# Batch-normalised matmul: chunk 11 of the turned x copied apart by GpSimd, one raw block of the third group sent the ordinary way

## The chip, the core and the metric

One core of one Trainium2 chip. The number that counts is the device time of one execution of the program, in microseconds (us). The core's engines are named as the profile names them: PE (TensorE, matmuls; PEld its weight loads), DVE (VectorE), ACT (ScalarE), POOL (GpSimd) and SP (SyncE, which only issues DMAs here). Matmuls write to PSUM, eight banks of 128 x 512 f32; everything else lives in SBUF.

## The reference

x is 16 x 512 x 1024, the weight 1024 x 768, both f32, so that y has 8192 rows and 768 columns. Every column is normalised over all 8192 rows:

```python
y = np.matmul(x, weight)
mean = np.mean(y, axis=(0, 1), keepdims=True)
var = np.var(y, axis=(0, 1), keepdims=True)
return (gamma * (y - mean) / np.sqrt(var + eps) + beta).astype(np.float32)
```

## The kernel before

**Tiles.** The 8192 rows are 16 chunks (c = 0 to 15) of 512 rows. The 768 columns are six tiles nt of 128. Tiles 0 and 1 are done together as the "first group" (256 columns, rows in the PSUM partitions, lines L509 to L671, for chunks 14 and 15 L813 to L826); tiles 2 to 5 are done one by one with the columns in the partitions, eight matmuls of 128 x 512 for each chunk (`col_unit`, L574). A tile can be normalised only when all 16 chunks of it have been multiplied and their statistics gathered, so its normalisation and its stores run beside the matmuls of the next tile, and only the last tile's stand alone at the end.

**x.** GpSimd issues the loads of x (L402), which cast it to bf16. VectorE turns each chunk (L427, L434) into a tile `xT_sb`, so that k lies in the partitions. In most chunks the turning moves 32-bit words, so that two neighbouring k (e = 0 and 1) stay side by side: the tile is `[P, JW, CH, 2]`, and a matmul on one e reads every second bf16 element. Chunks 2, 3 and 6 (`SINGLE`) are turned as single bf16 elements, slower on VectorE (L427), and are contiguous for each e. Chunks in `PARTED` (4, 5, 7 to 10) are copied apart by ScalarE (`part_chunk`, the copies are L546, four of 128 x 1024 for a chunk) into contiguous tiles `x_pl`. Chunks 12 to 15 (`LATE`) are copied apart just before tile 4, by VectorE or ScalarE, whichever the planner finds free. Chunk 11 isn't copied: tiles 2 to 5 read it from `xT_sb`. Chunks 0 to 3 are done for all tiles while x is still being loaded.

**After a matmul.** For a chunk of a tile, VectorE takes statistics (bn_stats, L710; for chunks 4 to 15 of tile 2 ScalarE does it instead, L719 and L723), and ScalarE moves y to SBUF as bf16 (L714), which frees the bank. The first group is summed by VectorE (L661, L665) and GpSimd (L665), merged (L794, L799), summed over the partitions on PE (L870), and brought to a scale and a shift: VectorE L879 to L882 (mean and variance of the sums), L820 (bn_stats of chunks 14 and 15), L886, ScalarE's root, then VectorE L893 to L898. PE spreads them over the partitions (L902). Two pairs of chunks' blocks (chunks 14 and 15) are then normalised by VectorE (L1063) and turned by PE (L1073); the other 14 by VectorE's product (L936) and an addition, on GpSimd for most (L941). GpSimd's additions of L665 and L799 are all that the change's words "behind its additions for the first group" mean.

**Tiles 2 to 4** go out in blocks of two chunks, in one of three ways. The ordinary way of tiles 2 and 3 (`col_block` in mode `xact`): normalise in place (ScalarE L1022 for tile 2, VectorE L1025 for tile 3), turn by a DMA transpose (L1219), ScalarE casts to f32 (L1231), SP stores (L1201). Tile 4 is normalised by VectorE too, and turned by PE between matmuls (L1043), cast by ScalarE (L1209). A *raw* block (`RAW`) is turned by DMA before it is normalised (L1105), for the chunks 0 to 3 while no store runs yet; once scale and shift are known they are spread along the free dimension (L1140 to L1157, seven small copies on GpSimd or ScalarE), VectorE multiplies (L1173), GpSimd adds (L1177), SP stores (L1181).

**The order.** Nothing is ordered by the hardware across engines but what semaphores say; on each engine, the order is fixed by `arrange`, a planner that runs when the program is built. It has a cost and a due time for each task and simulates the engines; a task may name two engines. Buffers (`Slot`) are given out in planned order from pools: eight banks, 12 places for `xT_sb` (`xts`), 29 for y (`ys`), 3 for squares (`sqs`), and a ring for x, turned blocks and results. So a small edit can reorder work far from it. `S` is the planned time at which the first group's matmuls end; `merges` are the last additions of the first group; `clock[0]` is the planned time of PE.

```python
def part_chunk(c, now, engines, small=False, step=0.0, after=()):
    slots = [Slot(sqs if jw < SQ else ys) for jw in range(JW)] if small else [Slot(xts)] * JW
```

A `small` copy lies in three places of `sqs` and one of `ys` in place of one whole `xts` place.

Of the kernel before, what the change touches and what calls it, by code (L numbers as in the profile page):

```python
# [227 lines left out]
def kernel(  # L228
# [20 lines left out]
    NT = N // P  # L249
# [3 lines left out]
    C = M // CH  # L253
# [9 lines left out]
    EARLY = 4  # L263
# [11 lines left out]
    PARTED, LATE, SINGLE = (4,5,7,8,9,10), (12,13,14,15), (2,3,6)  # L275
    MODE = {2:'xact',3:'xact',4:('pe',)*8}
    MODE = {nt: m if isinstance(m, tuple) else (m,) * (C // GY) for nt, m in MODE.items()}
    RAW, RAWADD, RAWDUE = {2:(0,2),3:(0,2),4:(0,2,4)}, {2:'POOL',3:'POOL',4:'POOL'}, {2:14.0,3:8.0,4:8.0}
    RING = 3 * CH // 32 * KQ // 2
    ENG = {"ACT": nc.scalar, "DVE": nc.vector, "POOL": nc.gpsimd, "SP": nc.sync}  # L280

# [11 lines left out]
    def seq(bi):  # L293

        ins = bi.ins
        prev = last.get(ins.engine)
        if prev is not None:
            tc.add_manual_dep(
                ins, prev,
                mybir.DependencyInfo(mybir.DependencyClass.NoSync, mybir.DependencyReason.DATA),  # L300
                reason="order",
            )
        last[ins.engine] = ins.name
        return bi
# [50 lines left out]
    def task(prio, engines, emit, deps=(), lock=False, **kw):  # L355
        t = Task(prio, engines, emit, deps, **kw)
        t.lock = lock
        tasks.append(t)
        return t
# [20 lines left out]
    w_ready, x_ready, x_slot, plain, last_loads = {}, {}, {}, {}, []  # L380
# [66 lines left out]
    for kind, n, *n1 in order:  # L447
# [24 lines left out]
        for i in range(rows // QR):  # L472
            c, q = divmod(m0 // QR + i, QPC)
# [9 lines left out]
        if rows % QR:  # L483
            t0 = rows // QR * QR // 32
            m1 = m0 + 32 * t0
            c, q = divmod(m1 // QR, QPC)
# [40 lines left out]
    def part_chunk(c, now, engines, small=False, step=0.0, after=()):  # L527

        src = x_slot[c]
        slots = [Slot(sqs if jw < SQ else ys) for jw in range(JW)] if small else [Slot(xts)] * JW  # L530
        ts = []

        def copy(jw):
            def emit(eng):
                if small:
                    if jw < SQ:
                        x_pl = sqpool.tile([P, 2, CH], bf16, tag="sq")
                    else:
                        x_pl = ypool.tile([P, 2, CH], bf16, tag="y")
                    slots[jw].tile = [x_pl]  # L540
                elif jw == 0:
                    x_pl = xtpool.tile([P, JW, 2, CH], bf16, tag="xT")
                    slots[0].tile = [x_pl[:, i] for i in range(JW)]
                dst = slots[jw].tile[0 if small else jw]
                pairs = src.tile[:, jw].rearrange("p m e -> p e m")
                seq(nc.scalar.copy(dst, pairs) if eng == "ACT" else ENG[eng].tensor_copy(dst, pairs))  # L546
            return emit

        for jw in range(JW):
            new = small or jw == 0  # L550
            ts.append(task(
                now + step * jw, engines, copy(jw), [x_ready[c, q, JW] for q in range(QPC)] + list(after) + ([] if new else ts[:1]),
                len(engines) > 1, uses=[src] + ([] if new else [slots[jw]]), takes=[slots[jw]] if new else []))
        plain[c] = slots, ts, small
# [71 lines left out]
    def col_unit(nt, c, jws, q0=0, q1=QPC):  # L626
        slot = bank_of.setdefault((nt, c), None) or Slot(banks)
        bank_of[nt, c] = slot
        first = jws[0] == 0 and q0 == 0
        xs = [plain[c][0][jw] for jw in jws] if c in plain else [x_slot[c]]  # L630
        kw = {"takes": [slot], "uses": xs} if first else {"uses": [slot] + xs}
        t = pe_task((1.728 if c in plain or c in SINGLE else 1.808) * len(jws) / JW * (q1 - q0) / QPC,
                    mm(nt, c, list(jws), slot, q0, q1),
                    waits(jws, c, q0, q1) + ([plain[c][1][jw] for jw in jws] if c in plain else []), (nt, c), **kw)
        if q1 - q0 == QPC:
            t.hosts = 4
        if jws[-1] == JW - 1 and q1 == QPC:
            col_stats(nt, c, slot, t)
        return t
# [60 lines left out]
    col_end = {}  # L700
# [88 lines left out]
    merges = []  # L789
# [70 lines left out]
    S = clock[0]  # L860
# [237 lines left out]
    def raw_turn(nt, c, due):  # L1098

        yslot, slot = y_of(nt, c), Slot(ys)  # L1100

        def xbar(eng):
            r_sb = ypool.tile([P, GY * RT, P], bf16, tag="y")
            slot.r = r_sb
            bi = nc.sync.dma_start_transpose(slot.r, y(nt, c, GY))  # L1105
            if not gated:
                tc.add_manual_dep(
                    bi.ins, gate.ins.name,
                    mybir.DependencyInfo(mybir.DependencyClass.Sync, mybir.DependencyReason.DATA),
                    reason="behind the loads",  # L1110
                )
                gated.append(bi)
            seq(bi)

        b = task(due, {"SP": (1.4, 1.4)}, xbar, [col_end[nt, c + i][1] for i in range(GY)] + [gate], dma=XBAR,
                 takes=[slot], uses=[yslot])
        raw[nt, c] = slot, b
# [8 lines left out]
    def raw_spread(nt, fin_task):  # L1126
        bank = Slot(banks)
        k = sorted(RAW).index(nt)
        acc, at = ((sum2, 0), (sum2, 2 * P), (sum3, 2 * P))[k]
        row = acc[:, at:at + 2 * P].rearrange("p (i n) -> p i n", n=P)  # L1130
        wide, turned = sum1[:, NA + 64 * k:NA + 64 * (k + 1)], sum3[:, 64 * k:64 * (k + 1)]
        both = turned.rearrange("p (i n) -> p i n", n=32)
        now = clock[0] + RAWDUE[nt] + 2.0

        def quadrant(i):
            return slice(32 * i, 32 * i + 32)

        def turn(eng):
            for i, src in enumerate((scale, shift)):
                seq(nc.vector.tensor_copy(wide[:, quadrant(i)], src[:, nt:nt + 1].to_broadcast([P, 32])))  # L1140
            seq(nc.vector.transpose(turned, wide))

        def move(eng, dst, src):
            seq(nc.scalar.copy(dst, src) if eng == "ACT" else nc.gpsimd.tensor_copy(dst, src))  # L1144

        def gather(eng):
            for i in range(4):
                move(eng, row[0:32, :, quadrant(i)], both[quadrant(i)])

        def deal(eng):  # L1150
            for i in range(1, 4):
                move(eng, row[quadrant(i)], row[0:32])

        def keep(eng):
            a_ps = psum.tile([P, CH], f32, tag="b")
            bank.tile = a_ps
            seq(nc.scalar.copy(a_ps[:, 0:2 * P], row.rearrange("p i n -> p (i n)")))  # L1157

        d = task(now, dve(0.35), turn, [fin_task], True)
        g = task(now, {"POOL": (0.8, 0.85), "ACT": (0.9, 1.0)}, gather, [d])  # L1160
        s = task(now, {"POOL": (1.2, 1.25), "ACT": (1.0, 1.1)}, deal, [g])
        t = task(now, act(0.4), keep, [s], takes=[bank])
        raw_aff[nt] = bank, t, s, row[:, 1]
# [97 lines left out]
    STEP = {2: 1.9, 3: 2.3, 4: 2.3}  # L1261
    CHUNKS = {nt: list(range(EARLY, C)) for nt in range(GA, NT)}
    if LATE:
        late = [c for c in range(EARLY, C) if c in LATE or c + 1 - c % 2 * 2 in LATE]
        rest = [c for c in range(EARLY, C) if c not in late]
        CHUNKS[NT - 3], CHUNKS[NT - 2] = late + rest, rest + late
    for nt in range(GA, NT - 1):
        if nt == NT - 2:
            for i, c in enumerate(LATE):
                part_chunk(c, clock[0] + 0.0 + 4.0 * i, {"DVE": (0.63, 0.7), "ACT": (1.05, 1.1)},  # L1270
                           i == 0, 4.0 / 4, [col_end[NT - 3, late[-1]][1]])
        for c in CHUNKS[nt]:
            for jws in halves if nt > GA or c > EARLY + 2 else [[jw] for jw in range(JW)]:
                col_unit(nt, c, jws)
        for c in RAW.get(nt, ()):
            if c >= EARLY:
                raw_turn(nt, c, clock[0])
        f = finish_tasks(nt)
        start = clock[0] + 3.0
        if nt in RAW:  # L1280
            raw_spread(nt, f)
        for i in range(C // GY):
            if (nt, GY * i) in raw:
                raw_block(nt, GY * i, start + STEP[nt] * i + RAWDUE[nt])
                continue
            if nt == NT - 2 and C // GY - HELD <= i:
                held.append((nt, GY * i, f))
                continue
            col_block(nt, GY * i, start + STEP[nt] * i, f)
# [121 lines left out]
```

## Time and profile before

| | us |
|---|---|
| median of 3 runs (lowest to highest) | 206.03 (205.75 to 206.65) |
| the profiled execution | 205.96 |
| its span, first to last instruction | 204.2 |
| PE busy | 191.0 (94%) |
| VectorE busy | 158.7 (78%) |
| ScalarE busy | 146.6 (72%) |
| GpSimd busy | 126.1 (62%) |
| mean granted TensorE clock | 0.975 |

The profiled execution took 1.76 us more than its span. All times of the trace are us from the start of the span. Lines (L574) are those of the kernel before; in the changed kernel, the lines from 279 to 1266 are numbered two higher, and those from 1267 on four higher.

### The profile page before, as it was taken

To read this page: it belongs to the slowest core of one execution; us is meant where nothing else is said; L and a number is where in the kernel's file an instruction comes from. 1 tells how busy PE (TensorE), PEld (TensorE's weight loads), DVE (VectorE), ACT (ScalarE), POOL (GpSimd) and SP (SyncE) were. 2 spreads that over 40 slices of the span, in tenths; PEclk is the share of its full clock that TensorE was granted. 3 is DMA by queue.
4 is the path that set the end of the run, shared out by engine and by line. 5 is a ranking of instruction groups with operands and counts; after the bars stand their busy time and mean duration, and the time that the engine had idled before them with its cause. 6 is when DMAs were issued, how large, how long until landed. Compare 5 with 4: busy or idle time off the path is not lost.

```text
span 204.2 us, 3509 instructions
## 1 busy us (share of the span) xinstructions
PE 191.0 (94%) x1210; PEld 116.3 (57%) x1210; DVE 158.7 (78%) x248; ACT 146.6 (72%) x261; POOL 126.1 (62%) x151
## 2 busy tenths in 40 slices
PE   7989999999999999999999999999999999996910
PEld 3467565656588888777875444444444445544810
DVE  4031979989999999969989998977999777937900
ACT  2001461468989999999978766999998969856950
POOL 7776964777399989997403999289616502850000
PEclk9999999999999999999999999999999999999685
DMA  4999999999999999999689999899999999999998
GB/s 73 168 200 196 181 196 196 196 198 197 189 194 197 197 199 194 196 197 195 93 187 214 334 339 336 242 306 326 316 291 201 334 322 244 347 343 310 309 347 249
DMA packets 98562, 48.74 MB, mean 239 GB/s; under 512 B 24304, under 2 KB 98032, under 8 KB 98544
## 3 DMA queue, kind: packets, MB, share of 16 engines
q0 software_dynamic: 34624, 18.36, 65.3%
q1 hardware_dynamic: 63920, 30.16, 53.7%
q8 instruction: 9, 0.15, 0.3%
q14 instruction: 9, 0.07, 0.1%
HBM read 36.71 MB, written 25.17 MB: 303 GB/s over the span
## 4 chain that ended last, share of the span: by engine, by line
PE 86%; ACT 3%; DMA 3%; POOL 2%; issue 1%; ACTq 0%; DVE 0%; POOLq 0%
PE y_ps L574 54%; PE y_ps L509 24%; PE y_ps L813 4%; ACT o_sb L1360 3%; DMA ring<-in_x_dram 3%; PE o_ps L1043 1%; POOL ring L402 1%; POOL w_sb L386 1%; PE y_ps L752 1%; PE a_ps L902 1%; PE o_ps L1073 0%; ACTq L1406 0%; PE idle_ps L590 0%; PE tot_ps L870 0%; ACT ring L1251 0%
## 5 line engine op out<-in xcount | busy, mean ns | idle before, releaser
L574 PEld LDWEIGHTS <-w_sb 128*128 128x128 bf16 x520 | 50.3, 97 | 57.6
L574 PE MATMUL y_ps<-xT_sb,w_sb 128*128 128x512 bf16 (+1 forms) x272 | 59.3, 371 | 0.0
L574 PE MATMUL y_ps<-x_pl,w_sb 128*128 128x512 bf16 x248 | 57.4, 379 | 0.0
L402 POOL DMA_DIRECT2D ring<-in_x_dram x76 | 47.3, 626 | 14.3 <-DMA ring<-in_x_dram 5.3
L509 PE MATMUL y_ps<-w_sb,xT_sb 128*128 128x256 bf16 x448 | 50.6, 273 | 0.7 <-DMA ring<-in_x_dram 0.6
L509 PEld LDWEIGHTS <-xT_sb 128*128 128x128 bf16 x448 | 43.5, 98 | 8.6 <-DVE xT_sb L434 2.1
L434 DVE STREAM_TRANSPOSE xT_sb<-ring 128x1024 f32<-128x1024 f32 (+1 forms) x29 | 31.2, 1112 | 14.1 <-DMA ring<-in_x_dram 14.0
L710 DVE BATCH_NORM_STATS2 stats<-y_ps 128x6 f32<-128x512 f32 x46 | 30.9, 687 | 8.6 <-PE y_ps L574 8.4
L546 ACT COPY x_pl<-xT_sb 128x1024 bf16<-128x1024 bf16 x34 | 34.8, 1063 | 1.7 <-DVE xT_sb L434 1.7
L714 ACT CAST y_sb<-y_ps 128x512 bf16<-128x512 f32 x51 | 28.7, 595 | 8.5 <-DVE stats L710 4.7
L941 POOL TENSOR_TENSOR ring<-ring,sum 128x1024 f32<-128x1024 f32 (+1 forms) x11 | 23.7, 2180 | 15.0 <-ACT y_ps L723 10.8
L658 ACT ACTIVATE sq_sb<-y_ps 128x512 f32<-128x512 f32 x28 | 16.4, 611 | 16.9 <-PE y_ps L509 16.4
L665 POOL TENSOR_TENSOR sum<-sum,sq_sb 128x512 f32<-128x512 f32 x20 | 25.6, 1280 | 3.1 <-ACT sq_sb L658 1.9
L661 DVE TENSOR_TENSOR sum<-y_ps,sum 128x512 f32<-128x512 f32 x28 | 18.9, 675 | 6.4 <-ACT sq_sb L658 5.3
L671 ACT CAST y_sb<-y_ps 128x512 bf16<-128x512 f32 x28 | 16.3, 593 | 8.3 <-DVE sum L661 8.0
L1177 POOL TENSOR_TENSOR ring<-ring,sum 128x1024 f32<-128x1024 f32 x7 | 17.1, 2469 | 4.5 <-issue 2.7
L936 DVE TENSOR_TENSOR ring<-y_sb,a_ps 128x1024 f32<-128x1024 bf16 (+1 forms) x16 | 16.7, 1080 | 0.1
L1144 POOL COPY sum<-sum 32x256 f32<-32x256 f32 (+1 forms) x17 | 5.5, 325 | 16.0 <-ACT sum L1144 9.2
L1043 PE MATMUL o_ps<-ident,y_sb 128*128 128x128 bf16 x104 | 13.7, 249 | 1.6 <-DVE y_sb L1347 1.5
L427 DVE STREAM_TRANSPOSE xT_sb<-ring 128x2048 bf16<-128x2048 bf16 x6 | 13.5, 2290 | 0.2 <-DMA ring<-in_x_dram 0.2
L1231 ACT CAST ring<-ring 128x1024 f32<-128x1024 bf16 x12 | 12.6, 1060 | 0.6 <-DMA ring<-y_sb 0.5
L590 PE MATMUL idle_ps<-idle_sb 128*128 128x512 f32 x18 | 10.5, 741 | 1.5 <-DVE idle_sb L316 1.5
(104 smaller groups left out, 154.9 us busy)
## 6 DMA issues: line engine op xcount, KB each, us to landing
out_dram<-ring SPq DMA_DIRECT2D x37, 512.0 KB, 3.5
ring<-in_x_dram POOLq DMA_DIRECT2D x52, 256.0 KB, 8.9
out_dram<-o_sb SPq DMA_DIRECT2D x6, 512.0 KB, 4.8
ring<-in_x_dram POOLq DMA_DIRECT2D x16, 128.0 KB, 5.8
w_sb<-in_weight_dram POOLq DMA_DIRECT2D x8, 192.0 KB, 6.2
out_dram<-ring SPq DMA_DIRECT2D x6, 256.0 KB, 3.1
ring<-in_x_dram POOLq DMA_DIRECT2D x4, 192.0 KB, 7.8
out_dram<-o_sb SPq DMA_DIRECT2D x3, 256.0 KB, 2.6
```

Source lines behind the costliest of these rows:

```text
L402: bi = seq(nc.gpsimd.dma_start(x_bf[32 * i:32 * i + 32], src[:, :, KQ * i:KQ * (i + 1)]))
L434: seq(nc.vector.transpose(dst, src[:, :, jw0:jw1]))
L509: seq(nc.tensor.matmul(y_ps[:, s], x_of(c, jw, e, t * P, (t + 1) * P), w_sb[:, jw, e, 0:NA], start=(s == 0 and jw == 0 and e == 0), stop=( ...
L546: seq(nc.scalar.copy(dst, pairs) if eng == "ACT" else ENG[eng].tensor_copy(dst, pairs))
L574: seq(nc.tensor.matmul(y_ps, w_sb[:, jw, e, nt * P:(nt + 1) * P], moving(c, jw, e, q0 * QR, q1 * QR, parted), start=(jw == 0 and e == 0 an ...
L661: seq(nc.vector.tensor_add(sum1, slot.tile[:, 0:n], sum1))
L665: seq(ENG[eng].tensor_add(acc, acc, state["sq"][:, 0:n]))
L710: seq(nc.vector.bn_stats(dst, slot.tile))
L714: seq(nc.scalar.copy(y(nt, c), slot.tile))
L936: seq(nc.vector.tensor_mul(slot.o, y_row[c].y[:, s0:s1], aff[0][:, None, :].to_broadcast([P, n, NA])))
L941: seq(ENG[eng].tensor_add(slot.o, slot.o, row[:, None, :].to_broadcast([P, n, NA])))
L1177: seq(ENG[eng].tensor_add(slot.o, slot.o, row[:, None, :].to_broadcast([P, n, P])))
```

## The change

Chunk 11 is added to the chunks that are copied apart, on GpSimd alone, after `merges`, in the small places that chunk 12 had; tiles 2 to 5 then read it from `x_pl`. Chunk 12's copies lie in an `xts` place instead. `LAST` holds the chunks that `LATE` held for the order of the chunks in tiles 3 and 4, which stays as it was. The raw block of chunks 2 and 3 of tile 2 leaves `RAW`: that block is now normalised first, by ScalarE, and goes the ordinary way.

```diff
-    RAW, RAWADD, RAWDUE = {2:(0,2),3:(0,2),4:(0,2,4)}, {2:'POOL',3:'POOL',4:'POOL'}, {2:14.0,3:8.0,4:8.0}
+    RAW, RAWADD, RAWDUE = {2:(0,),3:(0,2),4:(0,2,4)}, {2:'POOL',3:'POOL',4:'POOL'}, {2:14.0,3:8.0,4:8.0}
+    LAST = (12,13,14,15)
+    SOON = ((11, {"POOL": (1.06, 1.1)}),)
...
-        late = [c for c in range(EARLY, C) if c in LATE or c + 1 - c % 2 * 2 in LATE]
+        late = [c for c in range(EARLY, C) if c in LAST or c + 1 - c % 2 * 2 in LAST]
...
+    for i, (c, engines) in enumerate(SOON):
+        part_chunk(c, S - 60.0 + i, engines, i == 0, 0.1, list(merges) if i == 0 else plain[SOON[i - 1][0]][1][-1:])
     for nt in range(GA, NT - 1):
         if nt == NT - 2:
             for i, c in enumerate(LATE):
                 part_chunk(c, clock[0] + 0.0 + 4.0 * i, {"DVE": (0.63, 0.7), "ACT": (1.05, 1.1)},
-                           i == 0, 4.0 / 4, [col_end[NT - 3, late[-1]][1]])
+                           i == 0 and not SOON, 4.0 / 4, [col_end[NT - 3, late[-1]][1]])
```

The planner then gives another order. PE's order of matmuls is the same to the last one, with `x_pl` for `xT_sb` in 32 of them. On VectorE, five of the bn_stats of chunks 14 and 15 (L820) now stand ahead of L879 to L882, and both L886 behind the last of them; it makes 12 of the 16 copies of chunks 12 to 15 and ScalarE 4, where it was 6 and 10. ScalarE has one more normalisation (L1022) and one more cast (L1231), and takes the seven copies of one tile's spread (L1144) from GpSimd.

## The prediction

> **What bounds the kernel now.** I read the page's chain of waits first: it says what the end hangs on.
>
> ```profile
> PE 86%; ACT 3%; DMA 3%; POOL 2%; issue 1%; ACTq 0%; DVE 0%; POOLq 0%
> ```
>
> PE carries 86% of the span, and the windows show it without a gap from 12 to 186.5 us. So time is gained where a matmul gets shorter, and lost where PE has to wait for the first time. Next, PE's timeline in tile 3, for what a chunk costs in each layout of x.
>
> ```profile
> 132.58 1.89 PE L574 MATMUL y_ps<-xT_sb,w_sb 128*128 128x512 bf16 x8
> 134.31 7.07 PE L574 MATMUL y_ps<-x_pl,w_sb 128*128 128x512 bf16 x32
> 141.21 1.97 PE L574 MATMUL y_ps<-xT_sb,w_sb 128*128 128x512 bf16 x8
> 143.02 3.62 PE L574 MATMUL y_ps<-x_pl,w_sb 128*128 128x512 bf16 x16
> ```
>
> The distance between starts counts. Chunk 6 (turned as single elements, contiguous): 134.31 - 132.58 = 1.73 us. Four chunks of `x_pl`: 6.90, or 1.725 each. Chunk 11, interleaved: 143.02 - 141.21 = 1.81. Then the timelines where GpSimd will copy, and around the end of tile 4's statistics:
>
> ```profile
> 99.48 0.17 POOL L1319 COPY base<-beta_sb 128x1 f32<-128x1 f32 x1
> 110.50 2.50 POOL L941 TENSOR_TENSOR ring<-ring,sum 128x512 f32<-128x512 f32 x2 [10.84 <-ACT y_ps L723]
> ...
> 101.92 0.17 DVE L882 TENSOR_SCALAR gst<-msq 128x2 f32<-128x2 f32 x1
> 102.30 2.33 DVE L820 BATCH_NORM_STATS2 gst<-y_ps 128x6 f32<-128x256 f32 x6 [0.20 <-PE y_ps L813]
> 104.66 0.28 DVE L886 BATCH_NORM_AGGREGATE mv<-gst 128x2 f32<-128x27 f32 x1
> 105.01 0.43 DVE L820 BATCH_NORM_STATS2 gst<-y_ps 128x6 f32<-128x256 f32 x1
> 105.48 0.28 DVE L886 BATCH_NORM_AGGREGATE mv<-gst 128x2 f32<-128x27 f32 x1
> 106.32 0.16 DVE L894 TENSOR_TENSOR scale<-std,gamma_sb 128x2 f32<-128x2 f32 x1
> 106.60 0.52 PEld L902 LDWEIGHTS a_ps<-ident,scale 128*128 128x128 f32 x4 [0.39 <-issue]
> ...
> 168.09 0.53 DVE L1025 TENSOR_SCALAR y_sb<-y_sb,scale,shift 128x1024 bf16<-128x1024 bf16 x1
> 169.00 0.10 PEld L1043 LDWEIGHTS <-y_sb 128*128 128x128 bf16 x1
> ```
>
> GpSimd stands idle from 99.65 to 110.50. PE takes the first group's scale (L902) 0.12 us after VectorE has it (106.48), with nothing else put between; at 169.00 it takes tile 4's first normalised block 0.38 us after VectorE (168.62).
>
> **The saving.** 32 matmuls (8 for each of tiles 2 to 5) change from interleaved to contiguous: 4 x (1.81 - 1.725) = 0.34 us of PE time, all on the path. The Trainium skill, "SBUF — State Buffer", section "Door 1: The DMA port swizzle", says that SBUF is read in lines of 16 bytes, and that a bf16 operand may step by up to 8 elements at no cost. By that a step of two costs nothing and this term is 0; the rows above disagree, by 0.08 us per chunk.
>
> **The copies.** No row has GpSimd copying 128 x 1024 bf16. From below, its copies of f32:
>
> ```profile
> L1144 POOL COPY sum<-sum 32x256 f32<-32x256 f32 x9 | 3.7, 411 | 9.5 <-ACT sum L1144 9.2
> L1144 POOL COPY sum<-sum 32x64 f32<-32x64 f32 x8 | 1.8, 228 | 6.4 <-DVE sum L1141 6.2
> ```
>
> (411 - 228) / 192 = 0.95 ns an element, so 228 + 960 x 0.95 = 1.14 us. From above, its two-input addition on 128 x 1024, 2.38 us (L941). I take 1.14, since a copy reads one operand as L1144 does. Four take 4.6 us, from 99.4 (behind L799) to 104.0; at 2.38 they would end at 108.9. Both end before the idle time does and before the first matmul on them (112.86). For PE to wait for them there, each would have to take (112.86 - 99.4) / 4 = 3.4 us.
>
> **The first group's entry.** VectorE's order changes: five L820, then L879 to L882, two L820, two L886. The inputs come from PE every 0.91 us, the last at 104.98. The three transposes end at 101.45; the fifth L820 can end at about 103.6 (its matmuls end at 103.16); L879 to L882 take 0.71 (101.38 to 102.09 before), until 104.3; the last L820 still ends at 105.44, being PE's last product. But now both L886 come behind it: one more step of 0.24. The scale comes at 106.72, and PE had 0.1 us to spare: it waits 0.15 us (0, if the step overlaps, to 0.3). The chain behind (L893 to L898, L1063) moves along, so it is paid once.
>
> **VectorE in tiles 3 and 4.** Six copies more, at 0.69 (the median of L546 on VectorE): 4.1 us; one L1173 less, -1.2. In 139.4 to 165 it was busy 22.92 of 25.60 us, so +2.9 fills its 2.7 of idle time. I followed its order with these rows: tile 4's statistics, which PE's last product paces, still end near 164.6, but two L1025 and the aggregate behind them end 0.75 us later than before (166.1); the normalisation that PE needs at 169.0 then ends near 168.95, having been behind a bn_stats either way. I put 0.1 us of waiting there (0 to 0.6).
>
> **What costs nothing.** ScalarE gets 1.25 (L1022), 1.06 (L1231) and about 1.7 us of small copies (L1144), and loses six copies of 1.06: -2.3 us. It is full from 127 to 150, and the extra normalisation comes first; but a bank whose y it moves out about 2 us later is asked for only 4 to 5 us later. The raw block's L1177 (2.47 us) leaves GpSimd. SP has one DMA transpose less before the stores and one more among them, 1.7 us of issue; L945 behind it goes out that much later, and a ring place comes free later. DMA stands nearly idle at 171 to 173 (151 and 77 GB/s), so this backlog doesn't last. Chunk 12's copies need an `xts` place, and chunk 11's falls free at 104.
>
> **The end.** After PE's last product come the last statistics, then 4.2 MB of stores at 346 GB/s. Before it the store queue had run down to 195 GB/s at 188 to 189, so the end follows PE.
>
> **Sum.** -0.34 + 0.15 + 0.1 = -0.09. The profiled execution took 205.96 (span 204.2 and 1.76 around it), 0.07 below the median of the runs: 205.87 there, 205.9 in the runs. About 0.5% (1.0 us) is what a measurement of this kernel can tell from no change.
>
> **Rivals.**
>
> *GpSimd holds up the entry (slower).* GpSimd and VectorE exclude each other in some instructions:
>
> ```profile
> 141.19 5.17 POOL L1177 TENSOR_TENSOR ring<-ring,sum 128x1024 f32<-128x1024 f32 x2
> ...
> 145.85 0.54 DVE L992 SCALAR_TENSOR_TENSOR tmp<-mv,gamma_sb 128x1 f32<-128x1 f32 x1
> ```
>
> L992 on one element took 0.54 (0.16 at 165.37) and ended at 146.39, as GpSimd's addition did (146.36). L882 would stand near 104.2. If a copy takes over 1.2 us, the fourth is still running then, and the entry waits for it. At 1.4 us that is until 105.0, and the L820 left follow: 0.45 us more, 206.3. At 2.38, L882 meets a boundary, but L893 to L898 wait twice, 2.3 us: 208.2. Between: 207.2. For: VectorE has nothing else there. Against: 1.14 from the nearest rows. The Trainium skill, "SBUF — State Buffer", section "SBUF: two separate sides", calls this an exclusive lock, held for a whole instruction; by that rule a longer copy gives this rival, and the L992 row agrees.
>
> *VectorE becomes the bound at 169 (slower).* If its copies run beside GpSimd's additions they take 0.92 (143.23, during L1177) in place of 0.69: 6 x 0.23 = 1.4 us more, past the little that is left, so PE waits 1.3 us more: 207.2. It decides once VectorE slips by more than 0.4 us at 169. Against: GpSimd's spread for tile 3 goes to ScalarE, and its next addition waits for VectorE's product, so it should be idle through most of them.
>
> *Whole saving.* PE waits at neither place: 206.0 - 0.34 = 205.7. For: each wait is under 0.2 us.
>
> *The stores set the end.* If earlier casts close the gap at 171 to 173, about 1.4 us of DMA time, and the end is a matter of bytes: 206.0 - 1.4 = 204.6. Against: 188 to 189 was not full.
>
> *The copying saves nothing,* chunk 11 being slower for another reason than its layout: 0.15 + 0.1 = +0.25, 206.3. Chunk 6, contiguous without a copy and as fast as `x_pl`, speaks against it. The Trainium skill's rule on lines of 16 bytes (above) would give this.
>
> **Chances.** Forecast 0.50, whole saving 0.17, nothing saved 0.04 (all within 0.5%); GpSimd 0.11 and VectorE 0.12, of which 0.20 lie over 0.5% and 0.03 below; stores 0.06 (faster). So faster 0.06, same 0.74, slower 0.20. The range reaches from 205.2 (205.7 less the 0.28 by which the fastest run lay under the median, and a little of the stores' case) to 207.2, the value of both slower cases, half of which is so left out.
>
> **What would show it.** Right: four copies on GpSimd between 99.4 and 104; chunk 11 at 1.73 us in PE's timeline of tiles 2 to 5; a PE gap of 0.1 to 0.3 ahead of L902 (L904 there) and none or a small one at 169; the end of PE's products 0.1 us earlier. Wrong: copies over 1.2 us, an L882 (L884) that ends with one; PE waiting for VectorE's normalisation at 169; a wait of PE for a bank that ScalarE has not emptied; stores still queued when the last casts come.

## The result, and the profile after

The changed kernel takes 207.35 us (median of 7 runs, 206.73 to 208.26), the kernel before 206.03 (7 runs, 205.44 to 206.65): ratio 1.0074, 95% interval 1.0052 to 1.0095. It is slower by 1.3 us by the medians, 1.5 by the ratio, and above the range of the prediction. The profiled execution took 208.26 (span 206.5), 0.9 above its median: it is 0.59 us late already when the first group's scale reaches PE (L904 at 107.19, L902 at 106.60 before), because PE waited 1.4 us for the first x in place of 0.6. That part is the loads', not the change's.

The page's chain of waits after:

```profile
PE 79%; DMA 9%; ACT 3%; POOL 2%; DVE 1%; issue 1%; ACTq 0%; DVEq 0%; POOLq 0%
```

The 9% of DMA are the loads at the start (weights 6%, x 3%, in the row below it). At the end the chain runs through PE to ScalarE's last casts, as before. It doesn't show what makes the kernel slower: a store queue (the stores that are issued and not yet done) that stays full is no engine's wait.

The timelines of after where GpSimd copies, and in tile 3:

```profile
99.93 3.98 POOL L548 COPY x_pl<-xT_sb 128x1024 bf16<-128x1024 bf16 x4
...
104.14 0.14 DVE L881 COPY gst<-tot_ps 128x2 f32<-128x2 f32 x1
...
104.70 0.17 DVE L884 TENSOR_SCALAR gst<-msq 128x2 f32<-128x2 f32 x1
...
106.91 0.16 DVE L896 TENSOR_TENSOR scale<-std,gamma_sb 128x2 f32<-128x2 f32 x1
107.19 0.52 PEld L904 LDWEIGHTS a_ps<-ident,scale 128*128 128x128 f32 x4 [0.39 <-issue]
...
134.81 12.25 PE L576 MATMUL y_ps<-x_pl,w_sb 128*128 128x512 bf16 x56
146.90 0.38 PE L576 MATMUL y_ps<-xT_sb,w_sb 128*128 128x512 bf16 x1
```

The copies take 1.0 us each and end at 103.9, before L881 to L884, which aren't held up. PE takes the scale 0.12 us after VectorE has it, as before. Seven chunks in a row from `x_pl`, chunk 11 among them, take (146.90 - 134.81) / 7 = 1.727 us each. Then PE's products after the last chunk, first before, then after:

```profile
186.49 0.61 PE L1043 MATMUL o_ps<-ident,y_sb 128*128 128x128 bf16 x8
```

```profile
186.76 0.61 PE L1045 MATMUL o_ps<-ident,y_sb 128*128 128x128 bf16 x8
```

0.27 later after a start 0.59 later: PE gained 0.32 us, and it waits for nothing between 100 and 186. So up to here PE gained what the saving was forecast at, and everything that is lost comes behind PE, in the stores. The windows ahead of the end (us, PE, PEld, DVE, ACT and POOL busy, granted clock, DMA share, GB/s), before:

```profile
170.00:174.00 4.00, 4.00 (x31) 2.30 (x30) 2.65 (x5) 3.95 (x7) 1.35 (x3) 1.00 0.82 225
...
176.00:180.00 4.00, 4.00 (x25) 2.00 (x24) 2.75 (x5) 3.21 (x5) 4.00 (x3) 1.00 1.15 344
...
186.00:188.00 2.00, 1.10 (x14) 0.84 (x12) 1.25 (x6) 1.61 (x5) 0.00 (x0) 1.00 1.09 329
188.00:190.00 2.00, 1.33 (x15) 0.82 (x16) 1.96 (x7) 1.48 (x5) 0.00 (x0) 1.00 0.89 269
190.00:192.00 2.00, 2.00 (x24) 1.74 (x23) 2.00 (x8) 2.00 (x4) 0.00 (x0) 0.66 0.84 253
```

and after:

```profile
170.00:174.00 4.00, 4.00 (x32) 2.24 (x30) 2.80 (x6) 3.78 (x8) 1.18 (x3) 1.00 1.21 267
...
176.00:180.00 4.00, 4.00 (x27) 2.03 (x25) 3.59 (x5) 3.53 (x5) 3.74 (x3) 1.00 0.85 256
...
186.00:188.00 2.00, 1.37 (x17) 1.07 (x14) 1.27 (x4) 1.61 (x5) 0.00 (x0) 1.00 1.15 347
188.00:190.00 2.00, 1.06 (x12) 0.66 (x12) 1.89 (x8) 1.49 (x6) 0.00 (x0) 1.00 1.15 348
190.00:192.00 2.00, 2.00 (x22) 1.90 (x20) 2.00 (x8) 1.79 (x3) 0.00 (x0) 0.53 1.15 344
```

Read the last column against 346, the full rate. Before, the queue has a gap at 170 to 174, (346 - 225) x 4 / 346 = 1.40 us of its time, is full at 176 to 180 and runs dry at 186 to 192: (17 + 77 + 93) x 2 / 346 = 1.08 us to spare. After, the first gap is 0.91 us, a second one comes at 176 to 180, 90 x 4 / 346 = 1.04 us, and from there to the end the queue is full. The last 4 us in 40 slices of 0.1 us, before from 200, after from 202:

```profile
GB/s 348 343 348 353 338 338 343 348 353 348 343 348 353 348 343 348 353 348 343 328 348 353 348 343 348 353 333 108 26 0 0 0 0 0 0 0 0 0 0 0
```

```profile
GB/s 333 348 364 348 333 348 364 343 333 333 353 364 343 333 348 313 133 61 61 56 46 41 36 26 21 20 20 20 26 20 20 20 5 0 0 0 0 0 0 0
```

Before, the rate falls from 333 to nothing in 0.2 us, so the 16 DMA engines stop nearly together. After, they don't: in the 1.7 us after the last full slice the rate falls to 20, which is one engine of sixteen (346 / 16 = 21.6). So the full rate ends 0.9 us later, of which 0.6 is the late start, and the uneven end adds 1.5 us. A possible reason is in the DMA view of after at 180 to 182 (slices of 0.05 us):

```profile
GB/s 348 369 338 328 328 317 328 338 348 369 328 348 328 317 348 338 338 349 338 502 318 328 317 307 328 645 328 338 307 317 307 287 317 317 317 338 307 328 317 307
...
q8 instruction: 1, 0.02, 3.0%
```

The packet of a fetch of 16 KB of instructions is the peak of 645, near 181.3; right behind it the rate lies at some 315, one to two engines short. (A smaller packet of instructions, 8 KB on another queue, is the peak of 502 at 181.0; the rate is a little lower behind it already.) The kernel before has the same two packets near 179, and there the dry spell at 186 to 192 would give an engine that fell behind the time to catch up. What that looks like stands in its rates from 186 to 190, in slices of 0.1 us:

```profile
GB/s 338 348 353 338 343 338 348 358 348 338 348 353 353 338 348 353 353 338 272 77 46 128 41 41 67 241 348 353 343 343 353 353 333 328 338 353 353 343 343 338
```

From 187.9 to 188.5 two to four engines' worth still moves (41 to 77; the 128 holds another packet of instructions) while the others have nothing to do: so some engines were behind the rest. The trace doesn't say which engine moved a packet, so that they are behind because of the fetch is inferred here, and tested below (e9, e10, e13).

### The profile page after: what moved, and what is told of

It is laid out like the page before. It is cut to its first block, busy times and chain, and to the rows that moved or that the text cites. A ratio compares the mean times of both kernels' runs of the same rounds, so it can differ in the third digit from the quotient of the medians.

```text
span 206.5 us, 3514 instructions
## 1 busy us (share of the span) xinstructions
PE 190.0 (92%) x1210; PEld 116.5 (56%) x1210; DVE 160.1 (78%) x253; ACT 145.5 (70%) x264; POOL 125.3 (61%) x147
## 4 chain that ended last, share of the span: by engine, by line
PE 79%; DMA 9%; ACT 3%; POOL 2%; DVE 1%; issue 1%; ACTq 0%; DVEq 0%; POOLq 0%
PE y_ps L576 50%; PE y_ps L511 21%; DMA w_sb<-in_weight_dram 6%; PE y_ps L815 4%; DMA ring<-in_x_dram 3%; ACT o_sb L1364 3%; PE o_ps L1045 2%; POOL ring L404 1%; PE y_ps L754 1%; POOL w_sb L388 1%; DVE xT_sb L436 1%; PE a_ps L904 1%; PE o_ps L1075 0%; ACTq L1410 0%; PE tot_ps L872 0%
## 5 line engine op out<-in xcount | busy, mean ns | idle before, releaser
L576 PE MATMUL y_ps<-x_pl,w_sb 128*128 128x512 bf16 x280 | 63.8, 379 | 0.0
L576 PE MATMUL y_ps<-xT_sb,w_sb 128*128 128x512 bf16 (+1 forms) x240 | 51.6, 369 | 0.0
L548 ACT COPY x_pl<-xT_sb 128x1024 bf16<-128x1024 bf16 x28 | 28.8, 1061 | 1.7 <-DVE xT_sb L436 1.7
L1179 POOL TENSOR_TENSOR ring<-ring,sum 128x1024 f32<-128x1024 f32 x6 | 14.4, 2422 | 18.3 <-DVE ring L1175 18.3
L1233 ACT CAST ring<-ring 128x1024 f32<-128x1024 bf16 x13 | 13.6, 1057 | 0.2 <-DMA ring<-y_sb 0.2
L1045 PEld LDWEIGHTS <-y_sb 128*128 128x128 bf16 x104 | 8.9, 113 | 2.4 <-DVE y_sb L1351 1.9
```

The costliest lines, as they stand in the source:

```text
L576: seq(nc.tensor.matmul(y_ps, w_sb[:, jw, e, nt * P:(nt + 1) * P], moving(c, jw, e, q0 * QR, q1 * QR, parted), start=(jw == 0 and e == 0 an ...
L1045: seq(nc.tensor.transpose(dst, src, ident))
```

## The experiments

Theory A: VectorE's six extra copies make the last stores late. Theory B: the DMA transpose that now comes among the stores takes its DMA time. Theory C: chunk 11's copies cost it. Theory D: the block that now goes the ordinary way holds places of the ring, and tile 3's raw products wait for them. Theory L, formed after the first eight runs: the end is set by the last of 16 DMA engines, and they even out only where the queue runs dry. The table gives each run's ratio to the kernel before, measured beside it, and two values worked out from its profile: what was still to be moved at 180 us (the bytes of the 1-us windows from there on, over 346 GB/s, with the times shifted so that PE's first L902 or L904 falls together), and the uneven end (from the last slice of 300 GB/s or more to the last with any). The profiled executions of e11, e12 and e15 took 1.1 to 1.9 us more than their medians, so these two values are rough for them.

| | ratio (95% interval) | still to move at 180, us | uneven end, us |
|---|---|---|---|
| before | 1 | 21.7 | 0.2 |
| after | 1.0074 (1.0052 to 1.0095) | 23.2 | 1.7 |
| e1 chunk 11 alone | 0.9987 (0.9972 to 1.0002) | 21.5 | 0.6 |
| e2 raw block alone | 1.0081 (1.0058 to 1.0104) | 23.3 | 1.7 |
| e3 after, a transpose less | 1.0062 (1.0042 to 1.0082) | 22.4 | 1.5 |
| e5 after, cheap copies | 1.0041 (1.0025 to 1.0057) | 22.4 | 1.5 |
| e7 after, early normalisations | 1.0054 (1.0035 to 1.0072) | 23.1 | 1.7 |
| e8 after, a store less | 0.9984 (0.9969 to 0.9999) | 21.2 | 0.4 |
| e9 after, fetch earlier | 1.0035 (1.0020 to 1.0049) | 23.1 | 0.7 |
| e11 after, e3 and e5 | 1.0068 (1.0042 to 1.0094) | 23.5 | 1.9 |
| e12 before, a transpose more | 1.0037 (1.0015 to 1.0058) | 21.8 | 0.2 |
| e13 before, dry spell filled | 1.0041 (1.0026 to 1.0055) | 21.7 | 0.9 |
| e14 e1, fetch earlier | 1.0014 (0.9997 to 1.0031) | 21.5 | 0.6 |
| e15 after, casts earlier | 1.0041 (1.0028 to 1.0054) | 22.8 | 1.9 |
| e16 e1, a cast earlier | 1.0072 (1.0048 to 1.0095) | 22.9 | 1.8 |

**Which half of the change.** e1 is the kernel before with `SOON` and `LAST`, e2 with the `RAW` line alone:

```diff
-    RAW, RAWADD, RAWDUE = {2:(0,2),3:(0,2),4:(0,2,4)}, ...
+    RAW, RAWADD, RAWDUE = {2:(0,),3:(0,2),4:(0,2,4)}, ...
```

> The kernel before with chunk 11 copied apart by GpSimd as in the change, but both raw blocks of tile 2 kept. The planner gives VectorE 7 of the 16 copies of chunks 12 to 15 here (6 before, 12 in the changed kernel), and the stores see 12 DMA transposes, as before. Theory A (VectorE's extra copies make the last normalisations of tile 3 late, so two stores more are queued at 177 us): no slip, so only the saving of 0.3 us is left, 205.7. Theory B (the one DMA transpose more among the stores takes its DMA time, about 1.1 us by the three at 104 to 108 us of before): the same, 205.7. Theory C (GpSimd's copies of chunk 11 or their places cost it themselves): as the changed kernel, 207.3.

> The kernel before with the raw block of chunks 2 and 3 of tile 2 sent the ordinary way, and no copy of chunk 11. The planner gives VectorE 12 of the 16 copies, as in the changed kernel. Theory A: the changed kernel's loss without its saving, 207.6. Theory B: 207.4 to 207.6, too, one transpose more among the stores. Theory C: 206.0.

205.80 and 207.62. The raw block carries the whole loss, and chunk 11 alone costs nothing: it may gain the 0.2 to 0.3 us that its median and its ratio show, but its interval reaches 1. Theory C falls. e2's profile lies at its median (207.60) and has the same uneven end of 1.7 us, so this isn't owed to the slow profiled execution of the changed kernel.

**What makes the stores late.** e3 leaves out the transpose of the added block (its cast then reads the block unturned), e5 makes VectorE's copies contiguous, so that they no longer part the words, e11 does both:

```diff
-            seq(nc.sync.dma_start_transpose(t_slot.o, y(nt, c, GY)))
+            if (nt, c) != (2, 2):
+                seq(nc.sync.dma_start_transpose(t_slot.o, y(nt, c, GY)))
...
+                if eng == "DVE":
+                    dst, pairs = dst.rearrange("p e m -> p (e m)"), src.tile[:, jw].rearrange("p m e -> p (m e)")
```

> The changed kernel, with its order of instructions, but without the DMA transpose of the block of chunks 2 and 3 of tile 2, the one that came among the stores: the cast of that block reads the block as it was normalised, not turned. Its stores stay. Theory A: VectorE is as late as in the changed kernel, 207.1 to 207.3. Theory B: its DMA time of about 1.1 us comes back, 206.1 to 206.3.

> The changed kernel, same order and places, but each of VectorE's 12 copies of chunks 12 to 15 moves its 128x1024 words in the order in which they lie, contiguous on both sides, and not apart (so those chunks are wrong in tiles 4 and 5). An estimate is about half of 0.68 us for one, so VectorE gets some 4 us back between 142 and 158 us. Theory A (VectorE's lateness makes the stores late): the statistics and the root of tile 4 come about 1 us earlier, and the casts and stores behind them, 206.0 to 206.5. Theory D (it is the places of the ring: the block of tile 2 that now goes the ordinary way holds two of them in turn, and tile 3's raw products wait for these): the order and places are the same, so 207.2 to 207.4.

> The changed kernel with both reliefs that were tried apart: no DMA transpose of the block of chunks 2 and 3 of tile 2 (its cast reads the block unturned), and VectorE's 12 copies in the order in which the words lie (chunks 12 to 15 wrong in tiles 4 and 5). Each alone left the stores 0.7 us behind the kernel before at 180 us, where the changed kernel is 1.5 behind. If A and B add up (each took 0.8 us off), the queue is as far as before at 180, runs dry at 188 and lets the engines even out: 205.7 to 206.0. If each only laid bare the next limit (the ring): 206.6 to 207.0.

207.51, 206.99, 206.99. e5's copies took 0.41 us each in place of 0.68, so VectorE got 3 us back. Theory B gave next to nothing. Theory A gave 0.35 us of 1.3 by the medians, 0.7 of 1.5 by the ratios, with intervals that overlap; e5 lies between what the two theories expected. The two reliefs don't add up (e11). More telling is where the time stayed. By the table's sum, taken from 192 us on, e3 and e5 have 10.6 us left to move, less than the kernel before (10.8), and they still end uneven by 1.5 us: their stores left only 0.2 us unused between 180 and 192 (12 us less what was moved). e12 is B from the other side, on the kernel before:

```diff
+            if (nt, c) == (2, 4):
+                more = piece(slot)[:, 0:count * P // 2].bitcast(bf16).rearrange("p (s n) -> p s n", n=P)
+                seq(nc.sync.dma_start_transpose(more, y(nt, c, GY)))
```

> The kernel before with one DMA transpose more among the stores (the block of chunks 4 and 5 of tile 2 is turned a second time, into the place of the result, before the cast writes there); VectorE's work as before. Its DMA time of 0.74 (by its bytes) to 1.1 us is nearly what the queue had to spare at 187 to 192 (1.07 us). Theories B and L together: the queue hardly runs dry, the lagging engine keeps most of its 1.4 us, 206.4 to 207.2. If only late work of VectorE matters (A): 206.0.

206.53, in the range expected, but not for the reason: its queue is only 0.1 us behind at 180, runs dry as before and ends evenly. The gap at 171 to 173 took the transpose up. Its profiled execution reached the first group's scale 2 us late, after waits for x, so where the 0.5 us of its median go is open.

e4 and e6 give VectorE more copies in the order of before: e4 moves ScalarE's last six to it, e6 makes its own six twice.

```diff
+    late = [t for t in order if "part_chunk" in t.emit.__qualname__ and t.engine == "ACT" and len(t.engines) > 1]
+    for t in late[-6:]:
+        t.engine = "DVE"
```

> The kernel before with the last six of ScalarE's ten copies of chunks 12 to 15 given to VectorE at the same places of the planned order, so that it makes 12, as in the changed kernel; both raw blocks and the 12 DMA transposes among the stores stay. Theory A: the last normalisations of tile 3 come up to 4 us later, 207.0 to 207.4. Theory B: the stores are as before, 206.0.

> The kernel before, but VectorE makes each of its six copies of chunks 12 to 15 twice in a row: 6 x 0.69 = 4.1 us more of VectorE, as the change gives it, at the same places of the order and with the ring as before. Theory A: 206.7 to 207.4. Theory D: 206.0.

209.92 (1.0190, 1.0169 to 1.0211) and 210.31 (1.0204, 1.0180 to 1.0227): far more than A said, and with another mechanism, PE's waiting (2.2 us in e4, 2.9 in e6), here in the timeline of e4:

```profile
165.33 5.73 PE L574 MATMUL y_ps<-x_pl,w_sb 128*128 128x512 bf16 x18 [2.16 <-DVE x_pl L546]
```

Their stores are 4 us further back at 180 (25.7 and 25.9 us to move), but PE's waits stand ahead of them, so these two runs can't tell theory A from the rest. They price what the planner's new order avoids.

e7 moves VectorE's last normalisations of tile 3 ahead of its raw products, e15 two casts on ScalarE (`named` gives the tasks of a function in the planned order, `at` a task's tile and first chunk, `act` the first task on ScalarE planned after a time):

```diff
+    early = [t for t in named(".norm.") if at(t) in ((3, 12), (3, 14))]
+    first = next(t for t in named("norm_raw") if t.start > 155)
+    for t in early:
+        order.remove(t)
+    k = order.index(first)
+    order[k:k] = early
...
+    for cast, ahead in ((act("convert", 173.0), act("raw_spread.<locals>.keep", 172.0)),
+                        (act("convert", 176.0), act("col_stats.<locals>.keep", 175.0))):
+        order.remove(cast)
+        order.insert(order.index(ahead), cast)
```

> The changed kernel with one move in VectorE's order: the normalisations of chunks 12/13 and 14/15 of tile 3 (165.12 us, just ahead of tile 4's aggregate) stand ahead of the first raw product of tile 3 (158.74), where VectorE waited 0.29 and 0.41 us for places in the ring. Theory A: aggregate, root and the casts behind the root come 0.5 to 1 us earlier, 206.4 to 206.9. Theory D: the raw products come up to 0.7 later, 207.3 to 207.6.

> The changed kernel with one move in ScalarE's order: the casts of chunks 12/13 and 14/15 of tile 3 (173.25 and 175.86 us) each stand ahead of what waited for VectorE or GpSimd before them (the copy L1159 at 172.46, and the cast L716 at 175.38, which had waited 1.08 us). If the gap in the stores at 176 to 178 (1.04 us of DMA time) comes from these casts, it shrinks by 0.5 to 1.0 us, 206.5 to 207.0. If not: 207.2 to 207.4.

207.17 and 207.02. By the medians they recover 0.2 and 0.35 us, at the edge of what the intervals tell. e7 lies between its two expectations. e15 comes out at the edge of its first one, and the gap at 176 to 178 did shrink, to (346 - 295) x 2 / 346 = 0.3 us in its profile; but its end is as uneven as that of the changed kernel (1.9). What stood late can be read in VectorE's timeline, first before, then after:

```profile
154.85 1.20 DVE L1173 TENSOR_TENSOR ring<-r_sb,a_ps 128x1024 f32<-128x1024 bf16 x1
...
156.43 1.21 DVE L1173 TENSOR_TENSOR ring<-r_sb,a_ps 128x1024 f32<-128x1024 bf16 x1
...
161.18 1.45 DVE L1025 TENSOR_SCALAR y_sb<-y_sb,scale,shift 128x1024 bf16<-128x1024 bf16 x3
```

```profile
158.74 1.22 DVE L1175 TENSOR_TENSOR ring<-r_sb,a_ps 128x1024 f32<-128x1024 bf16 x1 [0.29 <-ACT ring L1233]
...
160.98 1.22 DVE L1175 TENSOR_TENSOR ring<-r_sb,a_ps 128x1024 f32<-128x1024 bf16 x1 [0.41 <-DMA out_dram<-ring]
...
165.12 0.98 DVE L1027 TENSOR_SCALAR y_sb<-y_sb,scale,shift 128x1024 bf16<-128x1024 bf16 x2
```

Tile 3's two raw products come 3.9 and 4.6 us later, behind VectorE's copies and then behind places in the ring; the last two normalisations come 3 to 4 us later. In each of these, 0.6 is the late start. With them, transposes, casts and GpSimd's additions move, and the stores come in another order and later. The waits for the ring (0.29 and 0.41 us) speak for theory D, but no run tries it by itself. Several of these stand behind one another; no single one was shown to carry the 1.5 us.

**What the late stores cost.** e8 leaves the store of chunks 10 and 11 of tile 4 out of the changed kernel, e9 shifts PE's instructions, e10 does so in the kernel before, e13 fills that kernel's dry spell (the remarks behind # are not in the code):

```diff
-            seq(ENG[eng].dma_start(dst(), slot.o))
+            if (nt, c) != (4, 10):                                                        # e8
+                seq(ENG[eng].dma_start(dst(), slot.o))
...
-            for _ in range(count):
+            for _ in range(count - 2 if count == WAKE else count):                        # e9; e10: 5
...
-            for _ in range(SMALL if count == WAKE else 0):
+            for _ in range(SMALL + 29 if count == WAKE else 0):                           # e9; e10: 72
...
-            seq(ENG[eng].dma_start(dst(), slot.o))
+            halves = 2 if nt == 4 and c in (8, 10) else 1                                 # e13
+            for h in range(halves):
+                part = slice(h * P // halves, (h + 1) * P // halves)
+                seq(ENG[eng].dma_start(dst()[:, :, part], slot.o[:, :, part]))
```

> The changed kernel without the store of chunks 10 and 11 of tile 4 (512 KB, issued at 183.03 us; these rows of the output stay unwritten). If the stores set the end, as both A and D say, its DMA time of 512 KB / 346 GB/s = 1.5 us comes off until the queue runs down as it did before at 188 to 192: 205.8 to 206.3. If PE and the last tile's own work set the end: 207.3.

> The changed kernel with 50 more instructions at the head of PE's stream, in the idle time of the start (two of the eight large warming matmuls left out, 29 small ones more): PE's last fetch of 16 KB of instructions, at 181.3 us, should come 50/256 of 25.7 us = 5 us earlier, at 176.3, ahead of the gap in the stores at 177 to 178. Theory L (the engine that carries this fetch falls 1.4 us behind with its share of the stores and catches up only when the queue runs dry, which it does at 187 to 192 before and no more after the change: the last 1.7 us of the changed kernel are one to three DMA engines): the gap of 1.0 us lets it catch up, so 206.0 to 206.5, and the stores end within 0.6 us on all engines. Without L (the end is the sum of the bytes): 207.3, as the changed kernel.

> The kernel before with 124 more instructions at the head of PE's stream, in the idle time of the start (five of the eight large warming matmuls left out, 72 small ones more), so that another fetch of 16 KB falls near 191 us, behind most of the time in which its store queue runs dry. Theory L: that engine ends 0.8 to 1.3 us behind the others, 206.8 to 207.3, with a tail of 20 to 40 GB/s. Without L: 206.0.

> The kernel before, but the stores of two blocks of tile 4 (chunks 8 to 11, about 177 to 182 us) are issued as two halves of 64 columns each, so that their packets are half as long and twice as many; PE, VectorE, ScalarE and GpSimd do what they did. How much longer such a store takes isn't known; an estimate from the two sides is 0 (same bytes) to 1.5 us each (same time for each packet), so the 1.07 us that the queue had to spare at 187 to 192 are used up if it is over 0.5 each. Theory L: without the dry spell the engine that carried PE's fetch at 179 stays 1.4 us behind, 206.8 to 208.0, with a tail of 20 to 60 GB/s. If the dry spell remains, or if it mattered only by its bytes: 206.0 to 206.4.

e8: 205.67, 1.7 us less for 1.5 us of bytes. The stores set the end of the changed kernel. In the profile the gain is less a matter of bytes (10.5 us left at 192 in place of 11.2) than of the end (uneven by 0.4 in place of 1.7): without that store the queue runs dry again, (346 - 276) x 6 / 346 = 1.2 us at 186 to 192. e9: 206.63, just above what theory L expected; its interval lies below that of the changed kernel, though its stores are no further on at 180. Its fetch came at 174.8, and of its gaps between 174 and 178 (257 GB/s there) most come behind the fetch. The last 4 us of its profile, from 201:

```profile
GB/s 348 333 348 358 353 328 353 358 353 328 353 358 353 328 333 348 364 348 333 348 343 169 67 51 36 20 20 15 0 0 0 0 0 0 0 0 0 0 0 0
```

1.7 us of uneven end became 0.7, and 0.7 us of the 1.3 are gone by the medians (0.8 of 1.5 by the ratios), though the stores' work is the same. The packet of 8 KB still came at 181.1, behind the gaps; whether the 0.7 that is left is its doing wasn't tried. e13: 206.91. Its windows show 348, 345 and 335 GB/s at 186 to 192, and its last 4 us, from 201:

```profile
GB/s 333 358 353 348 333 353 358 348 328 338 353 353 348 333 358 343 134 41 41 26 20 20 20 26 20 0 0 0 0 0 0 0 0 0 0 0 0 0 0 0
```

At 192 it has as much left to move as the kernel before (10.8 us, by the same sum), and its profile ends 0.9 us later with one engine behind. So a kernel with the same bytes left and no dry spell ends 0.9 us later, two thirds of what the change cost by the medians. The halved stores are a second difference, though: they run below the full rate themselves (272 GB/s at 180 to 185), so how much of the uneven end is theirs isn't separated. e10: 207.93, above what was expected. A further fetch came at 192.4 and its end is uneven by 1.0 us. Its stores also nearly stop, at 194 to 195 (33 GB/s; 10 to 20 in slices of 0.1 us, one engine at most), while SP's issue of the next store, at 192.60, lasts 1.77 us in place of 0.37 (before, at 191.66); and its profiled execution was 0.9 us late at the first group's scale. Only part of its 2 us is told by L; the rest is open.

The table as a whole agrees with L: the runs whose stores leave at most 0.3 us of the time between 180 and 192 unused (after, e2, e3, e5, e7, e11, e15, e16) end uneven by 1.5 to 1.9 us, those that leave about 1 us (before, e1, e8, e12, e14) by 0.2 to 0.6. Between them lie e9, with its fetch ahead of the gaps, e13, whose time to spare went into slower stores, and e10, with a fetch behind its dry spell.

The Trainium skill, "Runtime: NRT & Kernel Launch", section "Instruction fetch mechanics", says that instructions are refilled in blocks of 16 KiB, 256 instructions, and that crossing such a boundary costs one bump of a DMA tail, "mostly hidden". The trace agrees on the size (one packet of 0.02 MB). By 256 instructions to a block, an estimate is that e9's 50 move the fetch by 50/256 of the 25.7 us between two fetches, or 5 us; it moved by 6.5. For PE the fetch is hidden here: it waits for nothing from 100 to 186 us. For the stores it is so only while they leave gaps: e9 against the changed kernel, 0.7 us.

**The half that gained.** e14 is e1 with e9's shift, e16 is e1 with one cast moved on ScalarE:

```diff
+    cast, ahead = act("convert", 171.0), act("raw_spread.<locals>.gather", 168.0)
+    order.remove(cast)
+    order.insert(order.index(ahead), cast)
```

> Chunk 11 copied apart by GpSimd, both raw blocks kept (as in e1, 205.8), with the 50 more instructions at the head of PE's stream of e9, so that PE's last fetch comes 5 to 6.5 us earlier, near 173, in the dry spell that this order has at 171 to 173. Theory L: the last half microsecond at 20 GB/s of e1 shrinks, 205.4 to 205.7. Without L: 205.8, or up to 206.1 if the warming matmuls left out cost at the start.

> Chunk 11 copied apart by GpSimd, both raw blocks kept (as in e1, 205.8), with one move in ScalarE's order: the cast of chunks 10/11 of tile 3 (170.77 us in e1) stands ahead of the small copies of tile 4's spread (169.13). Its store should be issued near 170.8 in place of 171.84 and fill most of the dry spell that the store queue has at 171 to 173. Theory L: the queue is 0.5 to 1 us further on at 180, its dry spell at 187 to 192 is longer, the engine behind catches up in full, and the last 0.5 us of e1 at 20 GB/s go: 205.3 to 205.6. If PE's end alone sets e1's end: 205.8.

206.25 and 207.65, both outside what was expected. In e14 the fetch moved from 179.0 to 176.0 only, behind the gap that it was meant to precede, and the uneven end stayed at 0.6; nothing was gained. It also shows that the 50 instructions by themselves, with two warming matmuls less, make nothing faster, as e9's gain would need if L were wrong. e16's timeline of ScalarE:

```profile
169.94 1.04 ACT L1233 CAST ring<-ring 128x1024 f32<-128x1024 bf16 x1 [1.08 <-DMA ring<-y_sb]
```

The moved cast waited 1.08 us for its transpose, and the spread and the raw products behind it came later. The stores had their gap at 174 to 176 (73 GB/s), and were 1.4 us further back at 180 than in e1. No dry spell was left, the end was uneven by 1.8 us, and the kernel was 1.8 us slower than e1, though PE's last products began as in e1 and nothing of the raw block was changed. Moving one cast in ScalarE's order, 35 us before the end, cost as much as the whole change.

## Why the prediction was wrong

*The saving.* Right: -0.32 us at PE's end, forecast -0.34. Chunk 11 takes 1.727 us where it took 1.81. The Trainium skill's rule on 16-byte lines ("SBUF — State Buffer", section "Door 1: The DMA port swizzle"), by which a step of two bf16 elements is free, isn't borne out; with it goes the rival that copying saves nothing.

*The copies.* Right in place and end; 1.0 us each in place of 1.14. GpSimd holds nothing up, and the rival on it falls.

*The first group's entry.* Forecast +0.15, measured 0. The step of L888 overlapped: 0.40 for the two together.

*VectorE in tiles 3 and 4.* The slip was read rightly (tile 4's aggregate ended at 166.60, or 166.0 without the late start, forecast 166.1), and PE waited 0 in place of 0.1. The rival that VectorE becomes the bound at 169 falls as to place; e4 and e6 show that PE does wait where the planner hasn't made room. The error was to ask only PE about this slip. The statistics and normalisations that came late also feed the transposes, casts and stores.

*What costs nothing.* Here the forecast failed: the step that put the raw block's new way at nothing for the stores, because DMA stands idle at 171 to 173 and "this backlog doesn't last". That holds for one transpose by itself (e12: 0.1 us left at 180). But raw products, normalisations and casts came later too, so that stores were missing where the queue had room: 0.9 of the 1.4 us at 170 to 174 stayed idle, 1.04 more fell idle at 176 to 180, and at 180 the stores were 1.5 us behind.

*The end.* "The end follows PE" goes with the dry spell of the kernel before, a margin of 1.08 us that the prediction saw (195 GB/s at 188 to 189) and didn't size. The change put the stores 1.5 us back, more than the margin. In the profiles that costs 0.4 us in bytes (11.2 against 10.8 us left at 192) and 1.5 in the uneven end, about the 1.7 by which the spans differ without the late start (206.5 - 204.2 - 0.59). What PE saved no longer counts, since the end hangs on the stores (e8).

*The stores set the end.* This rival named the right place and gave it the wrong sign: it took the queue to be filled earlier, and it was filled later. The sum lacked a rival in which the dry spell is lost; its price was to be had from the same windows, though not that of the uneven end.

Open: which of the late operations is first, how much of the uneven end is the fetch's and how much that of other packets, and whether another order with one raw block less would keep the dry spell.

## What to carry to other kernels

Where stores follow the last product, size the store queue's dry spell ahead of the end in microseconds, and count every slip of an engine that feeds stores against it, even if PE never waits. The chain of waits doesn't show a full queue; the GB/s row does, and its last slices tell whether the DMA engines end together. A small edit that makes a planner reorder late work is priced by what is stored when, not by the work it adds.

## What was not expected of the hardware

When stores stand back to back, some DMA engine falls behind the others by more than a microsecond and stays behind until the queue runs dry: the uneven end is 1.7 us after, 0.2 before. By e9 a fetch of 16 KB of instructions carries about 1 us of that: with the fetch moved ahead of the gaps the uneven end is 0.7. GpSimd copies 128 x 1024 bf16 apart in 1.0 us.
